# Attention matmuls of a two-block model kernel: operands padded to 128 rows and over 64 columns

## The chip, the cores and the metric

The kernel runs on one core of one Trainium2 chip. The metric is the device time of one execution in microseconds, as the median of three runs. One execution was also taken by the hardware profiler; its span runs from the first to the last instruction.

The engines are TensorE (PE; its weight loads are listed apart as PEld), VectorE (DVE), ScalarE (ACT), GpSimd (POOL) and SyncE (SP, which issues the weight transfers). A matmul has a stationary operand, loaded first by a weight load, and a moving operand that is streamed through. The profile gives a matmul's shape as rows*columns of the stationary operand, then the output: `64*128 64x464` uses 64 rows of the array, 128 of its columns and streams 464 columns.

## What is computed

Two blocks on 512 tokens of 1024 features. The first one is the place of the change: it puts 16 learned tokens in front, normalizes, projects to queries, keys, values, a gated linear unit and two gates, runs differential attention beside a causal depthwise convolution of 31 taps, mixes both, and ends with a feed-forward part. The second block (two layers of convolution and retention) isn't touched.

```python
def _diff_attention(q, k, v, lam, cid):
    ...
        s = jnp.einsum('bqhmd,bkhmd->bhmqk', qb, kf)
        mask = cid[None, :] <= qc[:, None]
        p = jax.nn.softmax(jnp.where(mask, s, NEG_INF), axis=-1)
        a = p[:, :, 0] - lam * p[:, :, 1]
        return jnp.einsum('bhqk,bkhe->bqhe', a, vf)
...
o = _diff_attention(q, k, v, lam, cid)
y_att = (_rms(o, subln_w[l]) * (1.0 - lambda_init)).reshape(b, lp, ATT_V)
...
m = jax.nn.sigmoid(g_att) * y_att + jax.nn.sigmoid(g_conv) * y_conv
```

Eight heads have two maps each (m = 0, 1) of 64 features; the softmaxes of the two maps are subtracted. A query sees the keys of its own chunk of 64 tokens and of those before it.

## The kernel before

All inputs are float32. A product is split: an operand becomes a high part (float32r) and a low part (the rest), and three products high x high, low x high and high x low are added up (`proj`, line 149). The weights come tile by tile: SyncE transfers 512 KB, ScalarE makes the high part (line 137), VectorE the low part (line 138), three tiles ahead of their use.

Features lie on the partitions for the projections, so a head's query tile has map 0 on partitions 0 to 63 and map 1 on 64 to 127. For the scores, four transfers on GpSimd's queue copy the high part of each map onto both halves of the partitions (`qh`, line 479), and four more build `kk` (line 492): for map 0 the high part of the keys over the low part, for map 1 the low part over the high part. One matmul of 128 rows (`qh` on `kk`, lines 523 and 535) then adds high x high and high x low at once. The third product, the low part of the query on the high part of the key, has 64 rows only: partitions 0 to 63 for map 0, 64 to 127 for map 1 (`MAP`, lines 527 and 536).

The queries of a head are worked on in five tiles (`QT`): 66, 128, 128, 128 and 64 queries with 80, 208, 336, 464 and 528 keys. In tiles 0 to 3 the first rows must not see the last 64 keys; a matmul adds -1e30 there, with `ones_r` of 2 or 64 columns as the stationary operand (line 526). In tile 4 the scores of a map fill two pieces of 264 keys, so it takes four matmuls (lines 535, 536). Then VectorE takes the maximum (lines 529, 538), ScalarE the exponential (line 544), VectorE subtracts the maps (line 550), TensorE transposes the result block by block (line 554) and ScalarE copies it (line 557). The output is a sum over blocks of keys (line 565); float32 there makes two passes of each matmul. The last block has 16 keys, so 16 rows. A sum over the features of the squared output, for the norm, uses one column of ones (line 572) and is copied to one row of `ssq` for each head (line 574); head 7 uses all columns of ones.

In the same loop stand the projections of values, queries, keys and gates. The depthwise convolution is VectorE work (line 389), put behind the rest in priority, and so are the normalization of its result (`norm_1`, `norm_2`) and the last gates. After the heads come the convolution's output product (line 587) and, between its parts, two matmuls with `sel` that spread 1 / rms of a head over all partitions (line 596). A planner lays out each engine's order once, before the run; engines then work through their lists in order and wait for each other by semaphores.

Of the kernel before, what the change touches and what calls it, by code (L numbers as in the profile page):

```python
# [18 lines left out]
P = 128  # L19
# [43 lines left out]
def kernel(ctx, tc, hT, par, pos, decay, w1, w2, out):  # L63
# [11 lines left out]

    # ---------------------------------------------------------------- weights
    order = []
# [71 lines left out]
    def proj(ps, w, xh, xl, t0, n, nk=NK, first=True, last=True, late=0):  # L149
        """ps[128, n] (+)= w^T x over nk blocks of 128 rows, in three float32r passes; the last  # L150
        late blocks after all others."""
        wh, wl = w
        passes = ((wh, xh), (wl, xh), (wh, xl))
        steps = [(a, b, k) for r in (range(nk - late), range(nk - late, nk)) for a, b in passes for k in r]
        for i, (a, b, k) in enumerate(steps):
            PE.matmul(ps, lhsT=a[:, ks(k)], rhs=b[k][:, t0:t0 + n],  # L156
                      start=first and i == 0, stop=last and i == len(steps) - 1)
# [4 lines left out]

    # ---------------------------------------------------------------- constants
    pr = const.tile([P, NPAR], F32, name="pr")
# [17 lines left out]
    def later(steps, by=20000):  # L182
        """Steps that fill gaps: behind the others of the attention in the scheduler's eyes."""
        at_ = tc.cur_priority
        tc.cur_priority = at_ + by
        steps()
        tc.cur_priority = at_

    # ---------------------------------------------------------------- norms
    class SumSq:  # L190
        """Per lane sums of squares over feature tiles, as the tiles come."""

# [14 lines left out]
        def total(self, ps, c0, cn, more=None):  # L207
            """The sum over all features, on every partition, with the squares of one more tile."""
            PE.matmul(ps, lhsT=ones, rhs=self.acc[:, c0:c0 + cn], start=True, stop=more is None)
            if more is not None:  # L210
                sq = npool.tile([P, T1], F32, tag="ntmp", bufs=3, name=f"sqx_{self.tag}_{c0}")
                S.activation(sq[:, :cn], more, AF.Square)
                PE.matmul(ps, lhsT=ones, rhs=sq[:, :cn], start=False, stop=True)
            return ps

        def by_token(self, ps, t0, col):
            """The sums of 128 tokens, a token on each partition."""
            PE.matmul(ps[:, col:col + 2], lhsT=self.acc[:, t0:t0 + P], rhs=ones[:, 0:2], start=True, stop=True)
# [13 lines left out]

    # =============================================================== block 1
    mixs = ExitStack()
# [21 lines left out]
    for c0, cn in C528:  # L256
# [4 lines left out]
        if c0 == 0:  # L261
            nc.sync.dma_start(pr[:, 8:], par[:, 8:])
    # also as h w, without 1 / rms: the first products don't wait for it
    xu = [[hpool.tile([P, T1], F32R, tag=f"x{p}", name=f"xu{p}{k}") for k in range(NK)] for p in "hl"]
# [22 lines left out]

    # u carries 1 + tanh(x / 2) = 2 sigmoid(x), so the taps are halved
    cw = pr[:, PAR["conv_dw_w"]:PAR["conv_dw_w"] + 8 * CONV_K]
# [34 lines left out]

    # ---- attention
    atts = ExitStack()
# [25 lines left out]
    later(lambda_, LB)  # L352

    negrow = ap1.tile([P, 64], F32R, name="negrow")
    V.tensor_scalar(negrow, ones[:, 0:64], ident[:, 0:1], NEG, ALU.mult, ALU.mult)
# [3 lines left out]
    for i in range(2):  # L359
        v_ = ap1.tile([P, 5, 256], F32, name=f"v{i}")  # L360
        V.memset(v_[:, 4, :], 0.0)
        vt.append(v_)
    ql_t = []
    for i in range(1):
        q = ap1.tile([P, 2, TQ], F32R, name=f"ql{i}")
        ql_t.append(q)
    at = []
# [51 lines left out]
    V.tensor_scalar(subw, pc("subln_w"), 0.5 * (1.0 - LAMBDA_INIT), None, ALU.mult)  # L419
    sel = mpool.tile([P, 4, P], F32R, name="sel")  # L420
    for j in range(4):
        V.tensor_scalar(sel[:, j, :], ones, ident[:, 32 * j:32 * j + 1], None, ALU.mult)
    tgc = []
# [23 lines left out]
    def att_rstd(tags):  # L447
        """1 / rms of the outputs of some heads, a head on a row, in two parts."""
        hi, lo = [ap1.tile([P, T1], F32R, tag=tag, name=f"rstd_{tag}")[:, :TQ] for tag in tags]
# [3 lines left out]
    for h in range(HEADS):  # L453
# [3 lines left out]
        if h % 2 == 0:  # L457
            wa, wb = getw(), getw()
            for tb in range(5):
# [7 lines left out]
                S.copy(vt[(h // 2) % 2][:m, tb, :], ps)  # L467
        # q: the high parts of each map twice, on both halves of the partitions
        w = getw()
        qh = ap2.tile([P, 2, TQ], F32R, tag="qh", bufs=1, name=f"qh{h}")  # L470
        qf, ql = ql_t[0][:, 0], ql_t[0][:, 1]
        for i, (c0, cn) in enumerate(C514):
            ps = mmA(f"q{h}_{i}")[:, :cn]
            proj(ps, w, xh, xl, TQ0 + c0, cn)
            c = slice(c0, c0 + cn)
            split(ps, qf[:, c], ql[:, c])
        for m in range(2):
            for r in range(2):
                nc.gpsimd.dma_start(fv(qh[64 * r:64 * r + 64, m, :]), fv(qf[64 * m:64 * m + 64, :]))
        # k: high part over low part (map 0), low part over high part (map 1)  # L480
        w = getw()
# [33 lines left out]
        for t, (q0, qn, nkey) in enumerate(QT):  # L515
# [3 lines left out]
            if t < 4:  # L519
                ps = psS.tile([P, 2, 512], F32, tag="ps", name=f"s{h}_{t}")  # L520
                nw = nkey
                for m in range(2):
                    PE.matmul(ps[:qn, m, :nw], lhsT=qh[:, m, q0:q0 + qn], rhs=kk[:, m, :nw], start=True, stop=False)
                    # the first rows don't see the last block of keys: -1e30 there
                    hid = HALO if t == 0 else 64
                    PE.matmul(ps[:hid, m, nkey - 64:nkey], lhsT=ones_r[:, :hid], rhs=negrow, start=False, stop=False)
                    PE.matmul(ps[:qn, m, :nw], lhsT=ql[MAP[m], q0:q0 + qn], rhs=kk[MAP[m], m, :nw], start=False, stop=True)
                    pm.append(ps[:qn, m, :nkey])
                V.tensor_reduce(mx[:qn], ps[:qn, :, :nkey], AX.X, ALU.max)
            else:  # L530
                for m in range(2):
                    ps = psS.tile([P, 1024], F32, tag="ps", name=f"s{h}_{t}_{m}")
                    for c0, cn in C528:
                        o = 248 + c0
                        PE.matmul(ps[:qn, o:o + cn], lhsT=qh[:, m, q0:q0 + qn], rhs=kk[:, m, c0:c0 + cn], start=True, stop=False)
                        PE.matmul(ps[:qn, o:o + cn], lhsT=ql[MAP[m], q0:q0 + qn], rhs=kk[MAP[m], m, c0:c0 + cn], start=False, stop=True)
                    pm.append(ps[:qn, 248:248 + T1])
# [4 lines left out]
            for m in range(2):  # L542
# [8 lines left out]
                                   ALU.mult, ALU.subtract)  # L551
            ptr = psT.tile([P, 512], F32, tag="tr", name=f"tr{h}_{t}")
            for b in range(nb):
                PE.transpose(ptr[:, b * qn:(b + 1) * qn], at[t][:qn, b * P:(b + 1) * P], ident[:qn, :qn])
            src = ptr[:, :nb * qn].rearrange("p (b q) -> p b q", b=nb)
            aT, qo = (aTA, q0) if t < 2 else (aTB, q0 - 194)
            S.copy(aT[:, :nb, qo:qo + qn], src)

        for aT, q0, qn, blocks in (
            (aTA, 0, 194, ((0, 0, P), (1, 66, P))),  # L560
            (aTB, 194, 320, ((0, 0, P), (1, 0, P), (2, 0, P), (3, 128, P), (4, 256, META))),
        ):
# [8 lines left out]
            if h < HEADS - 1:  # L571
                PE.matmul(ps[0:1, :qn], lhsT=ones[:, 0:1], rhs=sq[:, :qn], start=True, stop=True)
                g, r = SSQ[h]
                S.copy(ssq[r:r + 1, q0:q0 + qn], ps[0:1, :qn])
            else:
# [4 lines left out]

    # ---- m = sigmoid(g_conv) * y_conv + sigmoid(g_att) * y_att, in og
    for n in range(NK):
# [28 lines left out]

    # ---- h = h + m @ w_out
    res, res2 = [], []
# [18 lines left out]

    # ---- FFN
    psF = ctx.enter_context(tc.tile_pool(name="psF", bufs=PSF[0], space=PSUM, reuse_waits="tile"))
# [24 lines left out]
    def rotary():  # L659
# [12 lines left out]
        for dst, q in ((sn, 0.0), (cs, 0.25)):  # L672
# [8 lines left out]
            S.activation(dst, dst, AF.Sin)  # L681
        # lower half negated: -x2 sin there, x1 sin on the upper half
        V.tensor_scalar(sn[0:64], sn[0:64], -1.0, None, ALU.mult)
# [51 lines left out]

    # =============================================================== block 2
    b2pool = ctx.enter_context(tc.tile_pool(name="b2pool", bufs=1, reuse_waits="tile"))

    # rstd of the layer's input norm: by token (rt) and on every partition (rs). The first layer's
    # input is the final norm of block 1, so its own norm's square of rstd is 1 / (b + eps (a + eps))  # L740
    # on the raw sums, a = mean h^2 and b = mean (h w)^2.
    for l in range(2):
# [38 lines left out]
        for h in range(HEADS):  # L781
# [38 lines left out]
            if h == 0:  # L820
                # as the halves of x come
                for c0, cn in HALF:
# [62 lines left out]
        for cc in range(NK):  # L885
            def ctile(tag, n=SEQ):
                # the first ones don't wait for the end of the retention
                if cc == 1 and tag == "yv":
# [76 lines left out]
        for n in range(NK - 2):  # L965
            job(n, 0, SEQ)
        # brings the table of Sqrt in ahead of the norm
        S.activation(tmp1, sso.acc[:, 0:1], AF.Sqrt)
# [84 lines left out]
```

## Time and profile before

| | |
|---|---|
| median of 3 runs | 1922.99 us (1922.12 to 1925.09) |
| span of the profiled execution | 1920.3 us |
| TensorE busy | 1898.4 us (99%), 11802 matmuls |
| weight loads busy | 1679.8 us (87%) |
| VectorE busy | 1303.0 us (68%) |
| ScalarE busy | 837.3 us (44%) |
| GpSimd busy | 76.3 us (4%) |
| chain that ended last | 97% TensorE |

Heads 0 to 7 and the mixing of both branches run from about 108 to 507 us, before them the gated linear unit, after them the output product, the feed-forward part and block 2.

How to read it: matmuls are pipelined, and the end of one is modelled, so its duration (say 0.28 us for 258 columns) is longer than the time it takes from its neighbours. The time a matmul takes in a stream is the distance from its start to the start of the next one. A line of the order of time that ends in x8 is eight matmuls in a row, and its first number is the start of the first. "idle before <-" in brackets is time in which that engine did nothing ahead of the instruction. The windows give the time in which an engine was busy in a stretch, and in brackets its instructions.

### The profile page before, as it was taken

How to read it: one execution, taken by the hardware profiler on the slowest of the kernel's cores; microseconds unless marked ns; L12 is line 12 of the kernel's file. 1: busy time of each engine (PE TensorE's matmuls, PEld its weight loads, DVE VectorE, ACT ScalarE, POOL GpSimd, SP SyncE). 2: the span in 40 equal slices, each digit the busy share in tenths (PEclk: the TensorE clock that was granted, in tenths of full speed). 3: DMA queues.
4: the chain of work that ended last, by engine and by line, in shares of the span. 5: the costliest groups of instructions: out<-in, count | busy, mean ns of one | idle time of the engine just before them, and what ended most of it. 6: DMA issues, size and time to landing. Idle time of an engine off the chain costs nothing.

```text
span 1920.3 us, 29228 instructions
## 1 busy us (share of the span) xinstructions
PE 1898.4 (99%) x11802; PEld 1679.8 (87%) x11802; DVE 1303.0 (68%) x2116; ACT 837.3 (44%) x1473; POOL 76.3 (4%) x123
## 2 busy tenths in 40 slices
PE   8999999999999999999999999999999999999997
PEld 7999888888999999988988888888898888888887
DVE  8998888667678777733588776454277877745424
ACT  7234454566345444433445553222255555422222
POOL 3000000110000000000000000000020000000000
PEclk9999999999999999999999999999999999999999
DMA  4232223332333222222223222222223222222221
GB/s 150 99 112 88 89 67 100 89 89 67 105 111 99 88 97 91 83 102 99 91 77 108 79 88 88 99 90 95 98 69 99 94 92 90 77 99 88 99 94 60
DMA packets 53047, 177.78 MB, mean 93 GB/s; under 512 B 6640, under 2 KB 10736, under 8 KB 52912
## 3 DMA queue, kind: packets, MB, share of 16 engines
q1 hardware_dynamic: 47696, 160.80, 25.2%
q0 software_dynamic: 5072, 15.10, 2.9%
q8 instruction: 93, 1.52, 0.3%
q14 instruction: 42, 0.34, 0.1%
q10 hardware_dynamic: 144, 0.00, 0.0%
HBM read 165.25 MB, written 2.10 MB: 87 GB/s over the span
## 4 chain that ended last, share of the span: by engine, by line
PE 97%; DVE 1%; ACT 1%; issue 0%; DMA 0%; POOL 0%; SPq 0%; DVEq 0%; POOLq 0%
PE up L156 13%; PE w L156 9%; PE dn L156 6%; PE rz L156 5%; PE cb L156 5%; PE cx L156 5%; PE cc L156 5%; PE cz L156 5%; PE rq L156 5%; PE rk L156 5%; PE rv L793 4%; PE v L466 3%; PE k L156 3%; PE q L156 3%; PE yc L156 2%; PE ga L156 2%
## 5 line engine op out<-in xcount | busy, mean ns | idle before, releaser
L137 ACT CAST wh<-wraw 128x1024 fp32r<-128x1024 f32 (+1 forms) x300 | 313.1, 1045 | 503.6 <-PE cx L156 69.0
L138 DVE TENSOR_TENSOR wl<-wraw,wh 128x1024 fp32r<-128x1024 f32 (+1 forms) x300 | 364.6, 1216 | 195.6 <-ACT wh L137 194.9
L389 DVE SCALAR_TENSOR_TENSOR y<-u,pr,y 128x514 f32<-128x514 f32 x240 | 170.2, 744 | 0.0
L156 PE MATMUL up<-xh_ffn,wh 128*128 128x258 f32 x704 | 99.0, 282 | 0.0
L156 PE MATMUL up<-xl_ffn,wh 128*128 128x258 f32 x704 | 98.6, 282 | 0.0
L156 PE MATMUL up<-xh_ffn,wl 128*128 128x258 f32 x704 | 98.5, 282 | 0.0
L156 PEld LDWEIGHTS up<-xh_ffn,wh 128*128 128x128 f32 x704 | 90.5, 189 | 0.1
L156 PEld LDWEIGHTS up<-xl_ffn,wh 128*128 128x128 f32 x704 | 90.4, 189 | 0.0
L156 PEld LDWEIGHTS up<-xh_ffn,wl 128*128 128x128 f32 x704 | 90.4, 189 | 0.0
L706 DVE SCALAR_TENSOR_TENSOR cv<-cg,pr,cv 128x256 f32<-128x256 f32 x176 | 83.8, 480 | 7.9 <-ACT cv L703 6.5
L703 ACT ACTIVATE cv<-cg,pr 128x256 f32<-128x256 f32 x88 | 52.8, 599 | 63.4 <-DVE cg L700 63.4
L156 PE MATMUL w<-ml,wh 128*128 128x512 f32 (+1 forms) x320 | 66.9, 350 | 0.0
L156 PE MATMUL w<-mh,wh 128*128 128x512 f32 (+1 forms) x320 | 66.6, 350 | 0.0
L156 PE MATMUL w<-mh,wl 128*128 128x512 f32 (+1 forms) x320 | 66.2, 349 | 0.0
L876 DVE RECIPROCAL rsq<-rsq 128x512 f32<-128x512 f32 x16 | 53.6, 3350 | 14.1 <-ACT rsq L875 14.1
L156 PEld LDWEIGHTS w<-mh,wh 128*128 128x128 f32 x320 | 52.6, 188 | 8.8
L156 PEld LDWEIGHTS w<-ml,wh 128*128 128x128 f32 x320 | 52.5, 188 | 8.8
L156 PEld LDWEIGHTS w<-mh,wl 128*128 128x128 f32 x320 | 52.2, 188 | 8.7
L700 DVE TENSOR_TENSOR cg<-up,rs_ffn 128x258 f32<-128x258 f32 x88 | 37.3, 425 | 12.8 <-PE up L156 12.7
L156 PE MATMUL dn<-dh,wh 128*128 128x512 f32 (+1 forms) x198 | 44.6, 365 | 0.0
L156 PE MATMUL dn<-dh,wl 128*128 128x512 f32 (+1 forms) x198 | 44.6, 365 | 0.0
L156 PE MATMUL dn<-dl,wh 128*128 128x512 f32 (+1 forms) x198 | 44.6, 365 | 0.0
(409 smaller groups left out, 4281.4 us busy)
## 6 DMA issues: line engine op xcount, KB each, us to landing
wraw<-w_in SPq DMA_DIRECT2D x160, 512.0 KB, 3.3
wraw<-w_up SPq DMA_DIRECT2D x44, 512.0 KB, 3.3
wraw<-w_out SPq DMA_DIRECT2D x40, 512.0 KB, 3.3
wraw<-w_v SPq DMA_DIRECT2D x24, 512.0 KB, 3.3
wraw<-w_down SPq DMA_DIRECT2D x16, 512.0 KB, 3.3
qh<-ql POOLq DMA_DIRECT2D x32, 128.5 KB, 2.8
wraw<-w_conv_out SPq DMA_DIRECT2D x8, 512.0 KB, 3.3
dc<-dec POOLq DMA_DIRECT2D x16, 256.0 KB, 3.1
```

What stands on the lines that cost most here:

```text
L137: S.copy(wh[:, :n], raw)
L138: V.tensor_tensor(wl[:, :n], raw, fv(wh[:, :n]), ALU.subtract)
L156: PE.matmul(ps, lhsT=a[:, ks(k)], rhs=b[k][:, t0:t0 + n], start=first and i == 0, stop=last and i == len(steps) - 1)
L389: V.scalar_tensor_tensor(ys[i][:, :TQ], src, wj, ys[i][:, :TQ], ALU.mult, ALU.add)
L466: PE.matmul(ps, lhsT=x, rhs=w, start=p == 0 and k == 0, stop=p == 2 and k == NK - 1)
L700: V.tensor_tensor(g, ps, rs[:, c * 256:c * 256 + 258], ALU.mult)
L703: S.activation(t, g[:, 0:256], AF.Identity, scale=pr[:, o:o + 1], bias=pc("ffn_dw_b", f))
L706: V.scalar_tensor_tensor(t, g[:, k:k + 256], pr[:, o:o + 1], t, ALU.mult, ALU.add)
L793: PE.matmul(ps, lhsT=xx, rhs=w, start=p == 0 and k == 0, stop=p == 2 and k == NK - 1)
L876: V.reciprocal(rr, rr)
```

## The change

The attention's matmuls are given 128 rows and over 64 columns:

- `ql`, the low part of the query, becomes two tiles of 128 partitions, one for each map, with zeros on the other map's half. The third product then runs over all rows of `kk`; the other half adds zero. VectorE makes the two halves in two instructions.
- The query tiles are two columns longer (zeros), so that tile 4 computes 66 rows of scores; only 64 are used.
- The stationary operand of the -1e30 matmul is `hide`: 64 columns of ones, 64 of zeros (for tile 0 its last 66 columns).
- Tile 4's transposes take 66 rows.
- The last block of keys in the output takes 128 rows; the rows beyond 16 are zero in both operands (the value tile is cleared there at the start).
- The sum of squares uses all 128 columns of ones; the head's row is then read out of the result.
- `sel` is made after the heads, in the buffer of `qh`.

```diff
+    hide = ap1.tile([P, P], F32R, name="hide")
+    V.tensor_copy(hide[:, 0:64], ones[:, 0:64])
+    zero(hide[:, 64:128])
...
+    qf = ap1.tile([P, TQ + 2], F32R, name="qf")
+    ql = ap1.tile([P, 2, TQ + 2], F32R, name="ql")
+    zero(qf[:, TQ:])
+    zero(ql[64:128, 0, :])
+    zero(ql[0:64, 1, :])
...
-            split(ps, qf[:, c], ql[:, c])
+            S.copy(qf[:, c], ps)
+            for m in range(2):
+                V.tensor_tensor(ql[MAP[m], m, c], ps[MAP[m]], fv(qf[MAP[m], c]), ALU.subtract)
...
-                    hid = HALO if t == 0 else 64
-                    PE.matmul(ps[:hid, m, nkey - 64:nkey], lhsT=ones_r[:, :hid], rhs=negrow, start=False, stop=False)
-                    PE.matmul(ps[:qn, m, :nw], lhsT=ql[MAP[m], q0:q0 + qn], rhs=kk[MAP[m], m, :nw], start=False, stop=True)
+                    hid = hide[:, 64 - HALO:] if t == 0 else hide
+                    PE.matmul(ps[:qn, m, nkey - 64:nkey], lhsT=hid, rhs=negrow, start=False, stop=False)
+                    PE.matmul(ps[:qn, m, :nw], lhsT=ql[:, m, q0:q0 + qn], rhs=kk[:, m, :nw], start=False, stop=True)
...
-                        PE.matmul(ps[:qn, o:o + cn], lhsT=qh[:, m, q0:q0 + qn], rhs=kk[:, m, c0:c0 + cn], start=True, stop=False)
-                        PE.matmul(ps[:qn, o:o + cn], lhsT=ql[MAP[m], q0:q0 + qn], rhs=kk[MAP[m], m, c0:c0 + cn], start=False, stop=True)
+                        PE.matmul(ps[:66, o:o + cn], lhsT=qh[:, m, q0:q0 + 66], rhs=kk[:, m, c0:c0 + cn], start=True, stop=False)
+                        PE.matmul(ps[:66, o:o + cn], lhsT=ql[:, m, q0:q0 + 66], rhs=kk[:, m, c0:c0 + cn], start=False, stop=True)
...
+            qw = max(qn, 66)
             for b in range(nb):
-                PE.transpose(ptr[:, b * qn:(b + 1) * qn], at[t][:qn, b * P:(b + 1) * P], ident[:qn, :qn])
+                PE.transpose(ptr[:, b * qw:(b + 1) * qw], at[t][:qw, b * P:(b + 1) * P], ident[:qw, :qw])
...
-            (aTB, 194, 320, ((0, 0, P), (1, 0, P), (2, 0, P), (3, 128, P), (4, 256, META))),
+            (aTB, 194, 320, ((0, 0, P), (1, 0, P), (2, 0, P), (3, 128, P), (4, 256, P))),
...
-                PE.matmul(ps[0:1, :qn], lhsT=ones[:, 0:1], rhs=sq[:, :qn], start=True, stop=True)
+                PE.matmul(ps[:, :qn], lhsT=ones, rhs=sq[:, :qn], start=True, stop=True)
                 g, r = SSQ[h]
-                S.copy(ssq[r:r + 1, q0:q0 + qn], ps[0:1, :qn])
+                S.copy(ssq[r:r + 1, q0:q0 + qn], ps[r:r + 1, :qn])
...
+    sel = ap2.tile([P, 4, P], F32R, tag="qh", bufs=1, name="sel")
+    for j in range(4):
+        V.tensor_scalar(sel[:, j, :], ones, ident[:, 32 * j:32 * j + 1], None, ALU.mult)
```

The lines that made `sel` before the heads are removed. The matmuls of the values' last 16 tokens keep their 16 columns. Comments are dropped as well.

## Rows read from the trace of the kernel before

**Rows 1.** Windows: stretch, its length, then busy time of each engine.

```profile
40.00:108.00 68.00, 68.00 (x564) 67.86 (x562) 64.87 (x100) 21.04 (x32) 0.00 (x0) 1.00 0.30 101
...
147.00:366.00 219.00, 219.00 (x1605) 191.57 (x1604) 184.48 (x349) 105.59 (x262) 20.45 (x40) 1.00 0.29 86
366.00:507.00 141.00, 140.94 (x1030) 125.69 (x1029) 95.62 (x185) 81.54 (x173) 9.29 (x18) 1.00 0.27 83
```

**Rows 2.** Chain of waits in order of time: start, length, what; feed-forward part.

```profile
560.93 246.40 PE up L156 x2059
```

**Rows 3.** Order of time on TensorE, a softmax tile of 464 keys: start, duration, what.

```profile
275.09 0.38 PE L523 MATMUL s<-kk,qh 128*128 128x464 f32 x1
275.30 0.19 PE L526 MATMUL s<-negrow,ones_r 128*64 128x64 f32 x1
275.43 0.47 PE L527 MATMUL s<-kk,ql 64*128 64x464 f32 x1
275.83 0.47 PE L523 MATMUL s<-kk,qh 128*128 128x464 f32 x1
276.14 0.19 PE L526 MATMUL s<-negrow,ones_r 128*64 128x64 f32 x1
```

**Rows 4.** The same stretch, weight loads.

```profile
275.09 0.14 PEld L526 LDWEIGHTS s<-negrow,ones_r 128*64 128x64 f32 x1
275.43 0.18 PEld L527 LDWEIGHTS s<-kk,ql 64*128 64x128 f32 x1 [0.20 <-issue]
```

**Rows 5.** Order of time on TensorE, matmuls of 128 columns in block 2.

```profile
986.10 0.28 PE L852 MATMUL st<-qh,kl 128*128 128x128 f32 x1
986.21 0.27 PE L852 MATMUL st<-ql,kh 128*128 128x128 f32 x1
```

**Rows 6.** Order of time on TensorE, tiles of 80 and 208 keys.

```profile
428.90 0.25 PE L527 MATMUL s<-kk,ql 64*66 64x80 f32 x1
429.08 0.36 PE L523 MATMUL s<-kk,qh 128*128 128x208 f32 x1
429.29 0.19 PE L526 MATMUL s<-negrow,ones_r 128*64 128x64 f32 x1
429.41 0.36 PE L527 MATMUL s<-kk,ql 64*128 64x208 f32 x1
429.70 0.39 PE L156 MATMUL gc<-xl_mix,wh 128*128 128x258 f32 x1
```

**Rows 7.** Order of time on TensorE, the tile of 528 keys.

```profile
202.94 0.28 PE L535 MATMUL s<-kk,qh 128*64 128x264 f32 x1
...
203.94 0.38 PE L156 MATMUL q<-xl_mix,wh 128*128 128x256 f32 x1
```

**Rows 8.** Order of time on TensorE, around a sum of squares.

```profile
297.86 1.13 PE L156 MATMUL k<-xh_mix,wh 128*128 128x264 f32 x8
298.93 0.70 PE L572 MATMUL pss<-osq,ones 128*1 128x320 f32 x2
299.55 1.24 PE L156 MATMUL k<-xh_mix,wl 128*128 128x264 f32 x8
```

**Rows 9.** Order of time on TensorE, an output over five blocks of keys.

```profile
204.16 2.46 PE L565 MATMUL po<-aTB,v 128*128 128x320 f32 x10
206.55 0.62 PE L156 MATMUL q<-xl_mix,wh 128*128 128x256 f32 x3
```

**Rows 10.** Order of time on TensorE, transposes of 64 rows.

```profile
231.38 0.52 PE L554 MATMUL tr<-ident,a 64*128 64x64 f32 x5
231.84 0.39 PE L156 MATMUL q<-xh_mix,wl 128*128 128x258 f32 x1
```

**Rows 11.** Groups on VectorE: shapes, count, busy us, mean ns.

```profile
L161 DVE TENSOR_TENSOR ql<-q,ql 128x258 fp32r<-128x258 f32 x8 | 3.3, 418 | 0.0
```

**Rows 12.** VectorE's waits, 147 to 366 us: us in total, times, longest.

```profile
DVE mx L529 <- PE s L527: 10.4, 14, 1.3
DVE mx L538 <- PE s L536: 5.8, 7, 2.0
```

More of the change, by code (lines that the diff above doesn't have):

```diff
@@ L362 @@
         vt.append(v_)
[L363 to L366, printed above, removed]
+    qf = ap1.tile([P, TQ + 2], F32R, name="qf")
[3 more added lines that the diff above has]
+    zero(ql[0:64, 1, :])
+    zero(ql[0:64, 0, TQ:])
+    zero(ql[64:128, 1, TQ:])
     at = []
@@ L419 @@
     V.tensor_scalar(subw, pc("subln_w"), 0.5 * (1.0 - LAMBDA_INIT), None, ALU.mult)
-    sel = mpool.tile([P, 4, P], F32R, name="sel")
-    for j in range(4):
-        V.tensor_scalar(sel[:, j, :], ones, ident[:, 32 * j:32 * j + 1], None, ALU.mult)
     tgc = []
@@ L469 @@
         w = getw()
-        qh = ap2.tile([P, 2, TQ], F32R, tag="qh", bufs=1, name=f"qh{h}")
-        qf, ql = ql_t[0][:, 0], ql_t[0][:, 1]
+        qh = ap2.tile([P, 2, TQ + 2], F32R, tag="qh", bufs=1, name=f"qh{h}")
         for i, (c0, cn) in enumerate(C514):
@@ L552 @@
             ptr = psT.tile([P, 512], F32, tag="tr", name=f"tr{h}_{t}")
+            qw = max(qn, 66)
             for b in range(nb):
-                PE.transpose(ptr[:, b * qn:(b + 1) * qn], at[t][:qn, b * P:(b + 1) * P], ident[:qn, :qn])
-            src = ptr[:, :nb * qn].rearrange("p (b q) -> p b q", b=nb)
+                PE.transpose(ptr[:, b * qw:(b + 1) * qw], at[t][:qw, b * P:(b + 1) * P], ident[:qw, :qw])
+            src = ptr[:, :nb * qw].rearrange("p (b q) -> p b q", b=nb)
             aT, qo = (aTA, q0) if t < 2 else (aTB, q0 - 194)
-            S.copy(aT[:, :nb, qo:qo + qn], src)
+            S.copy(aT[:, :nb, qo:qo + qn], src[:, :, :qn])
         for aT, q0, qn, blocks in (
             (aTA, 0, 194, ((0, 0, P), (1, 66, P))),
-            (aTB, 194, 320, ((0, 0, P), (1, 0, P), (2, 0, P), (3, 128, P), (4, 256, META))),
+            (aTB, 194, 320, ((0, 0, P), (1, 0, P), (2, 0, P), (3, 128, P), (4, 256, P))),
         ):
```

## The prediction

> **What bounds the kernel now.** I read the stretches first: in every stretch of the attention (108 to 507 us) TensorE is busy for all of it and its clock is granted in full, while VectorE, the next one, has gaps [rows 1]. So I asked what TensorE's time is made of, and for that the unit is not the busy time of a matmul (these overlap) but the distance from its start to the start of the next. The chain of waits gives the undisturbed price: 2059 matmuls of 258 columns in 246.40 us, 0.120 us each [rows 2]. The order of time of one softmax tile gives the disturbed one [rows 3]: a full-width matmul of 464 columns takes 0.21 us to the next start (275.09 to 275.30) when it comes after full-width work; the one with 64 rows takes 0.40 (275.43 to 275.83) for as many columns; and the next full-width one takes 0.31 (275.83 to 276.14) instead of 0.21. The weight loads say why [rows 4]: the load for the 64 columns of ones starts at 275.09, with the matmul before it still running, so it is hidden; the load for the 64-row matmul starts only at 275.43, together with its matmul, after 0.20 us in which no load ran. So a change of the number of rows costs two things, each way: the array runs empty (0.09 to 0.10 us), and the next weight load lies bare (0.10 us). A change to fewer columns alone (128 to 64) costs nothing that these rows show. The one exception is the one-column sum: there, too, both sides show the loss [rows 8].
>
> One floor limits what padding can gain: matmuls with few columns but 128 columns of weights come every 0.11 us [rows 5], the time of the load.
>
> **The change part by part.** "Before" is start to start; "after" is the undisturbed price: 0.12 for 258 to 264 columns, 0.21 for 464, 0.155 for 336 (between these two by columns), 0.11 wherever the floor is higher.
>
> 1. Scores of tiles 1 to 3: 8 heads x 2 maps x 3 = 48 groups of query high, ones, query low. Tile 3: low part 0.40 to 0.21, the exposed load after it 0.10 to 0, the ones 0.13 to 0.11 (128 columns of weights must now be loaded behind it): 0.31 saved [rows 3]. Tile 2 has the same losses at 336 columns: 0.31. Tile 1: 0.29 to 0.11 (floor), 0.21 to 0.11 for the next, 0.12 to 0.11: 0.29 [rows 5, 6]. Sum 16 x (0.31 + 0.31 + 0.29) = 14.6 us.
> 2. Tile 0 (66 queries), 16 groups: 0.18 for the low part and 0.10 bare behind it, where 429.08 to 429.29 is 0.21 and not 0.11 [rows 6]. After, the floor, since a full weight load follows: 0.11. Saved 0.17, sum 2.7 us. The first two of a group have 2 or 66 columns of weights now and 66 afterwards; I cost them at nothing (0.06 each way at most, half the floor, 1.0 us).
> 3. Tile 4 (64 queries), 16 groups of four: 202.94 to 203.94 is 1.00 us [rows 7] plus 0.10 bare behind; after, 4 x 0.12. Saved 0.62, sum 9.8 us.
> 4. The sums of squares of heads 0 to 6, 14 pairs, with 128 columns of weights in place of one: 0.09 in front (eight matmuls in 1.07 us, not 0.98), 0.09 in the pair (0.62 for two of 0.265), 0.10 bare behind as in rows 3 [rows 3, 8]. Saved 0.28, sum 3.9 us. The copy now reads row r instead of row 0: the same.
> 5. The output's last block, 8 times two passes of 16 rows: ten passes in 2.39 us [rows 9]; six of 320 columns at 0.265 and two of 192 at 0.16 leave 0.48 for these two. After, the floor twice, 0.22; bare load behind 0.10. Saved about 0.35, sum 2.8 us.
> 6. Transposes of tile 4, five each, 66 rows instead of 64: 0.46 now [rows 10], 0.09 in front, 0.10 behind. After 4 x 0.065 + 0.11 = 0.37 if their loads are as quick as now, 0.55 if the floor of rows 5 holds. Nearest is the same transpose two columns narrower, so 0.37: 0.28 saved, less where it follows 64-row work already: 2.0 us (0.6 at the other end).
>
> Sum 35.8 us of TensorE time; 33 to 37 with the ends above.
>
> What is added elsewhere: the low part of the queries is two subtractions on half the lanes instead of one; an instruction of 258 columns takes 418 ns [rows 11], and I take the same for half the lanes (less is possible), so 16 x 0.42 = 6.7 us of VectorE over the eight heads. Some 15 short fills of zeros at the start of the attention, 3 us by that row at most, once. The four queue-issued copies of a query tile stay four; a row is 8 bytes longer. They are issued on GpSimd's queue as before and still wait for both halves of the high part only. The selector for the norm moves behind the last scores, since it takes the query tile's buffer: four short VectorE steps, and its readers (14 pairs of matmuls between the products of the convolution) can't start before. These products can run in their place, so I cost it at nothing; if they were not there it would be about 2 us.
>
> What is late next. VectorE is busy 184.5 of 219 us between 147 and 366 us [rows 1], where the convolution fills its gaps. Five heads are computed there, so TensorE wants to save 5/8 of 35.8 = 22.4 us and VectorE gets 4.2 us more: 188.7 of 196.6 us, 96%. That is what it bears between 40 and 108 us (64.87 of 68, 95%) without TensorE stopping once [rows 1]. And 16.2 us of its idle time there is waiting for the scores that now come sooner [rows 12]. I take off 2 us here. After 366 us VectorE has 45 us to spare; there I take off 2.5 us, one head's gain on its scores, for the serial normalization of the convolution, which the first matmuls behind it need. Together 4.5 off: 31.3 us.
>
> Every later stage only starts earlier. 1920.3 - 31.3 = 1889.0 us of span; the median of the runs is 2.7 us above the span of the profiled execution, so **1891.7 us**.
>
> **The rivals.**
>
> VectorE becomes the bound of heads 0 to 4. For it: 96% leaves 7.9 us for all its waits on others. If only the waits on the scores vanish and all other idle time stays, VectorE needs 184.5 + 4.2 + (34.5 - 16.2) = 207 us, so 12 us are saved there instead of 22.4. Against: the convolution is filler, and 95% was borne before. With 2.5 off later: 35.8 - 10.4 - 2.5 = 22.9, **1900 us**.
>
> The change doesn't do what it says, and it is slower: a weight load stays uncovered whenever the array is still at work on the same rows, so that padded matmuls lie as bare as now. Its place is the 64 groups of scores and the 28 sums; its price is that the padded loads are longer, 64 or 127 more columns at 0.11 per 128: 64 x 0.055 + 28 x 0.11 = 6.6 us, with nothing gained: **1930 us**. It decides if full-width loads aren't hidden behind full-width matmuls. Against it stands [rows 4]: at 275.09 a load on all 128 rows runs under a matmul on all 128 rows. The Trainium skill has this rule, on the page "TensorE: Matmul & The Clock Gate", section "What overlaps and what doesn't": weight loads overlap running matmuls only when their row groups differ. By it, padding to all rows would be the wrong thing, and the loads of rows 2 would be bare at every matmul; this trace shows them hidden there (0.120 us start to start), so I give it little. The same page's other sentence (Part 2, step 1), that a load may also go to a background buffer, is the one these rows bear out.
>
> The order of the instructions is planned anew, and a wait lands where there was none (the scores behind their copies, the selector). Its price lies between the selector's 2 us and VectorE's 10 us above, off the gain, 1894 to 1902 us.
>
> **How the numbers follow.** Forecast 0.62 (1884 to 1894 us); VectorE as the bound 0.20 (1895 to 1903); new order 0.11; slower 0.04; the rest, half of the gain or less, 0.03. The range leaves out the slower case and the rest: its low end is 37 us saved and nothing lost (1886) with 3 us for an order that comes out better, its high end the second and third case with some of both, 1905. A measurement can tell about 0.2% (4 us) from no change; faster 0.93, same 0.03, slower 0.04.
>
> **What would show it.** Right: in one softmax tile of the changed kernel, the low part of 464 columns at about 0.21 us to the next start and no idle time before its weight load; tile 4's four at 0.49; attention some 31 us shorter; everything from 507 us on as long as before. TensorE's idle time inside the attention, now none, says how much VectorE or the new order gave back: under 5 us if I am right, over 10 if VectorE binds, with the transposes, the weights' low parts or the scores waiting for VectorE. Wrong: a load that still starts with its matmul.

## The result and the profile after

| | before | after |
|---|---|---|
| median | 1923.43 us (1922.12 to 1925.09, 4 runs) | 1901.85 us (1900.37 to 1902.45, 4 runs) |
| span of the profiled execution | 1920.3 us | 1900.5 us |
| TensorE busy | 1898.4 us (99%) | 1869.6 us (98%) |
| VectorE busy | 1303.0 us (68%) | 1312.2 us (69%) |

The ratio is 0.9889, 95% interval 0.9875 to 0.9903: 21.6 us faster. The range (1883 to 1905) holds the time. The likeliest case (31.7 us off, its own range 1884 to 1894) did not come; 1901.85 lies in the places of two rivals, VectorE as the bound (1895 to 1903) and a new order (1894 to 1902). The time alone can't tell them apart; the waits below do.

**The padding does to TensorE what the steps say.** Order of time on TensorE in the kernel after, a tile of 464 keys (start, duration, what), the counterpart of [rows 3]:

```profile
378.40 0.37 PE L529 MATMUL s<-kk,qh 128*128 128x464 f32 x1
378.60 0.19 PE L532 MATMUL s<-negrow,hide 128*128 128x64 f32 x1
378.63 0.45 PE L533 MATMUL s<-kk,ql 128*128 128x464 f32 x1
378.93 0.37 PE L529 MATMUL s<-kk,qh 128*128 128x464 f32 x1
```

378.40 to 378.93 is 0.53 us for a group; 275.09 to 275.83 in [rows 3] was 0.74, with the bare load behind it still to come. The forecast was 0.21 + 0.11 + 0.21. The ones take 0.03 and the low part 0.30: the floor is paid in another place, the sum is the same. The weight loads of the same tile, the counterpart of [rows 4], have no idle time before them:

```profile
378.40 0.19 PEld L532 LDWEIGHTS s<-negrow,hide 128*128 128x128 f32 x1
378.61 0.19 PEld L533 LDWEIGHTS s<-kk,ql 128*128 128x128 f32 x1
```

Tile 4, the counterpart of [rows 7], and a sum of squares, that of [rows 8], both on TensorE:

```profile
278.83 0.28 PE L541 MATMUL s<-kk,qh 128*66 128x264 f32 x1
278.95 0.28 PE L542 MATMUL s<-kk,ql 128*66 128x264 f32 x1
279.07 0.29 PE L541 MATMUL s<-kk,qh 128*66 128x264 f32 x1
279.19 0.28 PE L542 MATMUL s<-kk,ql 128*66 128x264 f32 x1
279.31 0.87 PE L156 MATMUL q<-xh_mix,wl 128*128 128x256 f32 x6
...
282.06 0.28 PE L156 MATMUL k<-xh_mix,wl 128*128 128x264 f32 x1
282.18 0.70 PE L579 MATMUL pss<-osq,ones 128*128 128x320 f32 x2
282.48 1.25 PE L156 MATMUL k<-xh_mix,wl 128*128 128x264 f32 x7
283.57 1.12 PE L156 MATMUL k<-xl_mix,wh 128*128 128x264 f32 x8
```

Four matmuls in 0.48 us (1.00 before), and the pair of the sum takes 0.30 to the next start (0.62 before). But that is not all of its price: the seven matmuls behind it take 1.09 us to the next start (282.48 to 283.57), where seven at 0.12 are 0.84. So some 0.25 us of the pair's time shows behind it, and it costs about 0.54. Before, it cost 0.62 and the 0.09 in front and 0.10 behind that the prediction names. So it saves about 0.28, as forecast, and not 0.32. The undisturbed price of the feed-forward part is what it was, as the chain of waits says:

```profile
541.85 246.40 PE up L156 x2059
```

**TensorE now stands still.** Windows of after (stretch, length, then busy us and instructions of PE, PEld, DVE, ACT, POOL; granted clock, DMA share, GB/s), to be held against [rows 1]; the last two rows are two stretches in which the granted clock was at the lower level, 1.2 GHz:

```profile
147.00:366.00 219.00, 218.01 (x1775) 212.38 (x1774) 202.73 (x388) 117.61 (x292) 24.54 (x48) 1.00 0.32 98
366.00:507.00 141.00, 133.19 (x1025) 128.43 (x1024) 99.14 (x193) 81.42 (x163) 6.79 (x13) 0.96 0.25 80
...
232.00:317.00 85.00, 85.00 (x684) 82.43 (x683) 81.41 (x156) 43.93 (x111) 8.17 (x16) 1.00 0.30 94
...
395.60:402.40 6.80, 5.78 (x23) 5.06 (x24) 3.81 (x3) 4.60 (x7) 0.00 (x0) 0.50 0.23 77
426.30:429.70 3.40, 3.40 (x18) 3.40 (x18) 3.40 (x6) 2.27 (x7) 0.00 (x0) 0.50 0.12 25
```

Before, TensorE never waited between 100 and 500 us. After, its waits there are these (us in total, times, longest). `gc` and `ga` are the projections of the two gates, `tgc` and `tga` what ScalarE makes of them, `lnv` the sum for the variance of the convolution's normalization, `rs_ln` one over its root, and `yc` the convolution's output product:

```profile
PE yc L156 <- ACT tgc L439: 2.7, 1, 2.7
PE lnv L209 <- ACT rs_ln L221: 2.2, 1, 2.2
PE yc L156 <- DVE tgc L599: 2.1, 2, 1.4
PE tr L561 <- ACT aTA L564: 1.0, 1, 1.0
PE gc L156 <- ACT tga L448: 0.5, 1, 0.5
PE pss L579 <- DVE og L576: 0.3, 1, 0.3
```

All but the 1.0 us lie behind 392 us, in the serial normalization of the convolution (`norm_2`) and what follows. Order of time on TensorE there:

```profile
392.18 0.60 PE L209 MATMUL lnv<-acc_ln,ones 128*128 128x258 f32 x2
393.11 0.81 PE L579 MATMUL pss<-osq,ones 128*128 128x320 f32 x2 [0.32 <-DVE og L576]
396.14 1.22 PE L209 MATMUL lnv<-acc_ln,ones 128*128 128x256 f32 x2 [2.23 <-ACT rs_ln L221]
397.83 2.09 PE L156 MATMUL gc<-xh_mix,wh 128*128 128x258 f32 x8 [0.48 <-ACT tga L448]
399.72 1.92 PE L156 MATMUL gc<-xh_mix,wl 128*128 128x258 f32 x8
...
425.54 1.51 PE L156 MATMUL yc<-xh_u,wh 128*128 128x258 f32 x8 [2.67 <-ACT tgc L439]
```

`norm_2` works on two halves of 258 and 256 tokens. Before, both sums were four matmuls in a row at 420.02. In the new order the second half comes 3.96 us behind the first, has to wait until ScalarE has read the first, and ScalarE reloads its table for it. ScalarE in that place:

```profile
394.31 1.28 ACT L221 ACT_TABLE_LOAD   x1
395.61 0.48 ACT L221 ACTIVATE rs_ln<-lnv,epsc 128x258 f32<-128x258 f32 x1
396.10 1.28 ACT L448 ACT_TABLE_LOAD   x1
397.40 0.66 ACT L448 ACTIVATE tga<-ga 128x258 f32<-128x258 f32 x2
398.08 0.42 ACT L581 COPY ssq<-pss 1x320 f32<-1x320 f32 x1
398.52 1.28 ACT L221 ACT_TABLE_LOAD   x1
399.81 0.48 ACT L221 ACTIVATE rs_ln<-lnv,epsc 128x256 f32<-128x256 f32 x1
```

The clock falls to half 1.7 us into the stand of 2.23 us, at 395.60, for 6.8 us: the eight `gc` matmuls at 397.83 take 1.89 us to the next start, where eight of 0.12 are 0.96. From the first `lnv` to the first `yc` it was 25.1 us (420.02 to 445.12), and is 33.4.

The longest stand, 2.67 us ahead of `yc`, ends with this instruction on ScalarE:

```profile
425.10 0.40 ACT L439 ACTIVATE tgc<-gc 128x256 f32<-128x256 f32 x1
```

`yc` doesn't read `tgc`, so what it waits for must be one of the three buffers that the projections share. In ScalarE's order that instruction stands behind eight casts of the normalized convolution, from 419.52 on, and the high part of a weight tile at 424.15.

**Where the 19.8 us of span come from.** Worked out from TensorE's order of time, first `v` to first `wo`, each matmul by the distance to the next start, idle time apart. The two columns on the right are two kernels of the last experiments, whose edits differ in the padding alone.

| us | before | after | g4 (not padded) | f1 (padded) |
|---|---|---|---|---|
| scores and -1e30 | 55.0 | 32.9 | 55.0 | 32.8 |
| `po` | 23.0 | 20.4 | 23.3 | 20.4 |
| `pss` | 7.8 | 4.4 | 7.8 | 4.2 |
| transposes | 9.8 | 8.6 | 10.0 | 8.7 |
| projections, norms, `rb`, `yc` | 303.4 | 303.5 | 307.0 | 300.5 |
| TensorE idle | 0.1 | 8.8 | 2.2 | 1.3 |
| sum | 399.1 | 378.6 | 405.3 | 367.8 |

Before to after, TensorE's work shrinks by 29.2 us (399.0 to 369.8, unrounded). That holds the loss from the clock: 5.78 us of busy time at 395.6 and 3.40 at 426.3, half of each lost, an estimate of 4.6 us. So the padding gave 33.8 us. Against it stand 8.7 us of added idle time, the 4.6 us, and 1.4 us lost at the start (first `v` at 109.71, not 108.30); later stages are 0.7 us shorter. 33.8 - 8.7 - 4.6 - 1.4 + 0.7 = 19.8.

### The profile page after: what moved, and what is told of

The parts are those of the page before. It is cut to its first block, busy times and chain, and to the rows that moved or that the text cites. A ratio compares the mean times of both kernels' runs of the same rounds, so it can differ in the third digit from the quotient of the medians.

```text
span 1900.5 us, 29258 instructions
## 1 busy us (share of the span) xinstructions
PE 1869.6 (98%) x11802; PEld 1683.7 (89%) x11802; DVE 1312.2 (69%) x2147; ACT 838.8 (44%) x1475; POOL 75.0 (4%) x123
## 4 chain that ended last, share of the span: by engine, by line
PE 95%; DVE 2%; ACT 1%; issue 1%; POOL 0%; DMA 0%; SPq 0%; DVEq 0%; ACTq 0%; POOLq 0%
PE up L156 13%; PE w L156 9%; PE dn L156 6%; PE rz L156 5%; PE cb L156 5%; PE cx L156 5%; PE cc L156 5%; PE cz L156 5%; PE rq L156 5%; PE rk L156 5%; PE rv L804 5%; PE v L471 3%; PE gc L156 3%; PE k L156 2%; PE wo L156 2%; PE q L156 2%
```

## The experiments

The first theory: the padding's gain is on TensorE in full, and the lost part is the planner's new order around the convolution's normalization, with the clock that falls behind the stands. The second: VectorE, at up to 96% in heads 0 to 4, gives back what TensorE gains. The medians of the kernel before beside these runs were 1922.1 to 1922.9 us.

**Without the normalization of the convolution.** In four kernels `norm_1` and `norm_2` are left out (n1: before, n2: after, n3: only the score lines padded, n4: only the sums, the last block and the transposes).

```diff
-            later(norm_2, N2)
...
-            later(norm_1, N1)
+            pass
```

> The kernel before without the layer norm and SiLU of the convolution branch (its products take the raw convolution), so that no serial chain stands between the last head and those products. The convolution on VectorE stays. First theory (TensorE's gain from padding is there in full, and what is missing is lost at that chain): about 1910 to 1920 us, since TensorE was busy all the time before and only four float32 pairs of matmuls go. Second theory (VectorE's longer work eats the gain): says the same of this one. It is the base of the next three.

> The changed kernel without that layer norm and SiLU. First theory: 33 to 36 us below n1 (the sum of TensorE's terms was 35.8), TensorE idle under 2 us in the attention. Second theory: still 19 to 23 us below n1, since the convolution and the second subtraction are both still VectorE's, with TensorE waiting for VectorE in heads 0 to 4.

> As n2, with the sums of squares, the last block of keys and the transposes of the last tile as before: only the scores are padded. First theory: 27 us below n1 (terms 14.6, 2.7, 9.8), 25 to 29. Second theory: 12 to 17, since all of VectorE's added work is here.

> As n1, with only the sums of squares (128 columns), the last block of keys (128 rows) and the transposes of the last tile (66 rows) padded; VectorE's work is as before. First theory: 8.7 us below n1 (terms 3.9, 2.8, 2.0), 7 to 10. Second theory: the same, as nothing is added on VectorE. If the one-column sum lost its time to something other than its columns, 4 us less.

Measured: n1 1921.07 us (ratio 0.9991, 0.9982 to 1.0000), n2 1890.71 (0.9832, 0.9816 to 0.9848), n3 1901.08 (0.9887, 0.9872 to 0.9902), n4 1912.74 (0.9949, 0.9935 to 0.9964). n1 is 1 us above the 1910 to 1920 that was expected. Leaving the normalization out gains nothing that can be measured in the kernel before and 11.1 us after. With it gone the padding is worth 30.4 us: less than the first theory's 33 to 36, far more than the second's. In n2 TensorE is idle for 3.9 us in the attention (under 2 were expected), and the clock does not fall there. By the tally, idle time left out, TensorE's work shrinks by 33.4 us from n1 to n2. n3 (20.0 below n1) lies between what both theories say: its work shrinks by 24.0 us, and it is idle for 4.2, the most of it for ScalarE's copies behind the transposes. n4 (8.3) is where it was expected, but n1 has a spell of 3.4 us at half clock at 1433 us that n4 has not, which makes up to 1.7 of it. So these four point at the stretch; they do not settle the size.

**One reciprocal root for both halves of the variance (f1), another place for the gates' products (f2), both (f3), and f2's edit in the kernel before (f4).** f1 also takes the sum out of the projections' buffers into one of the scores'. `GC_EARLY` is the number of heads that do one of the eight `gc` products each; the other products come at the end.

```diff
-        for i, (c0, cn) in enumerate(C514):
-            ps = mmA(f"lnv{i}")[:, :cn]
-            rstd(rs[:, c0:c0 + cn], ss.total(ps, c0, cn), D, epsc[:, 1:2])
+        ps = psS.tile([P, 1024], F32, tag="ps", name="lnv")
+        for c0, cn in C514:
+            ss.total(ps[:, 254 + c0:254 + c0 + cn], c0, cn)
+        rstd(rs[:, :TQ], ps[:, 254:254 + TQ], D, epsc[:, 1:2])
```

```diff
-GC_EARLY = 5
+GC_EARLY = 4
```

> The changed kernel; the variance of the layer norm is summed for all 514 tokens into one buffer of the scores instead of two of the three buffers of the projections, and its root and reciprocal are one instruction each instead of two. First theory (the gain is lost at the serial chain of the layer norm, where TensorE stands for 2.2 and 0.5 us and then runs at half clock for 6.8 us): 5 to 7 us below the changed kernel, 1895 to 1897 us, with no gap of over 1 us at the variance. Second theory (VectorE's longer work): within 2 us of the changed kernel.

> The changed kernel with GC_EARLY = 4 instead of 5: the gate projection of head 4 is done at the end, where it can run while the layer norm's chain is waited for. TensorE has the same work. First theory: the gap of 2.7 us ahead of the convolution's products goes, and the 1.7 us at half clock behind it: 1896 to 1899 us. Second theory: VectorE has 5.7 us less of TensorE's time in heads 0 to 4 to hide in, so no gain or up to 5 us slower.

> f1 and f2 together. First theory: both gains, 1890 to 1894 us, within 4 us of the changed kernel without the layer norm (1890.7). Second theory: as f2.

> The kernel before with GC_EARLY = 4. TensorE had no gap there, so by the first theory nothing is gained by the constant alone: within 2 us of 1922.4. If f2 gains and this one as much, the gain of f2 is not that of the gap.

Measured: f1 1890.17 us (0.9828, 0.9814 to 0.9843), f2 1895.74 (0.9856, 0.9841 to 0.9871), f3 1903.20 (0.9894, 0.9879 to 0.9909), f4 1930.76 (1.0042, 1.0028 to 1.0057). **f1 beats both kernels**: 32.7 us below before, 11.7 below after. That is 5 us more than the first theory gave it, since not only the stand at the variance went. f1's one stand of TensorE between 100 and 500 us (us in total, times, longest) and its sums in the order of time:

```profile
PE tr L562 <- ACT aTA L565: 1.0, 1, 1.0
...
391.25 1.03 PE L209 MATMUL lnv<-acc_ln,ones 128*128 128x258 f32 x4
```

Both halves stand in one row again, and the first `yc` comes at 413.93 instead of 425.54. In f1 the clock falls nowhere between 14.4 and 1881.5 us. VectorE is as busy in heads 0 to 4 as in after (its windows, 232 to 317 us), and TensorE has no gap beside it:

```profile
232.00:317.00 85.00, 85.00 (x686) 82.51 (x685) 81.35 (x158) 44.41 (x113) 8.16 (x16) 1.00 0.30 94
```

f2 gains 6.1 us, as the first theory had it. Its halves are parted too, the second `lnv` 3.98 us behind the first, but TensorE stands for 0.91 us only, and the clock doesn't fall there. So the cost is in the stands and the clock, not in the parting as such.

f3 and f4 missed. f3 has both edits and is slower than either, and than after: its halves stand in one row, but there are new gaps of 1.1, 1.7 and 1.4 us at 394, 440 and 467 us. So one root doesn't protect from a bad order elsewhere. f4, where one constant differs, is 7.9 us slower than before: its order also parts the two halves, with a stand of 1.89 us ahead of the second and 6.8 us at half clock from 419.7 us. So that order is no property of padded matmuls: a small edit elsewhere can bring it.

**What else the change touches: columns without rows (g1, on f1), VectorE's added work without the padding (g2, on before), f1's edit in the kernel before (g3), and g2 with that edit (g4).**

```diff
-                    PE.matmul(ps[:qn, m, nkey - 64:nkey], lhsT=hid, rhs=negrow, start=False, stop=False)
+                    PE.matmul(ps[:hid, m, nkey - 64:nkey], lhsT=hide[:, :hid], rhs=negrow, start=False, stop=False)
...
-                PE.matmul(ps[:, :qn], lhsT=ones, rhs=sq[:, :qn], start=True, stop=True)
+                nc_ = 64 if h < 4 else 16
+                PE.matmul(ps[:nc_, :qn], lhsT=ones[:, :nc_], rhs=sq[:, :qn], start=True, stop=True)
```

(g1; tile 4's matmuls go back to `q0:q0 + qn` in the same way. g2 has the diff of the change but for its matmuls, so `lhsT=ql[MAP[m], m, q0:q0 + qn], rhs=kk[MAP[m], m, :nw]`, 64 rows, the one-column sums, 16 rows in the last block and 64-row transposes.)

> The changed kernel with one reciprocal root for both halves of the variance, in which the row padding stays (low part of the queries, last block of keys, transposes) and the column padding is taken back: 64 columns again for the -1e30 matmul (2 in tile 0) and for tile 4's scores, and for the sums of squares 64 columns in heads 0 to 3 and 16 in heads 4 to 6. If only the rows matter, as the rows of before suggest for 64 columns: tile 4's four matmuls still come at 0.12 us each, the -1e30 matmul between its neighbours costs no more than with 128 columns, the pair of a 64-column sum costs 0.30 us as with 128 and that of 16 columns too or up to 0.28 us more; time 1890 to 1894 us, against 1890 for the same kernel with all columns. If columns under 65 cost like rows: 0.2 us for each of 64 groups of scores or 28 sums, so 1900 to 1908 us.

> The kernel before with only the work that the change puts on VectorE: two subtractions per query piece in place of one, the fills of zeros, the selector made behind the heads; all matmuls as before. If VectorE's added work costs nothing, as the gap-free heads 0 to 4 of the changed kernel say: within 4 us of before (a new order may add or take that much). If VectorE was short: 5 to 10 us slower, with TensorE's waits for VectorE in heads 0 to 4.

> The kernel before with one reciprocal root for both halves of the convolution's variance, nothing else. If the 12 us that this edit gains in the changed kernel are the stands that its order had there, it gains nothing here, where TensorE has none: within 3 us of before. If the edit is worth as much by itself: 1909 to 1913 us, and the changed kernel's lost part isn't explained by its order.

> The kernel before with the change's work on VectorE (as g2_vector_side_only, 1936.1 us) and one reciprocal root for both halves of the variance (which gained nothing in the kernel before: 1921.9 us). If the change's lost part is the place where its order puts the two halves of the variance, the 14 us of g2 go away here as 12 us went away in the changed kernel: 1920 to 1926 us, and the padding alone is worth what lies between this and the changed kernel with one root, 32 to 34 us. If the added work on VectorE, or the later selector, costs by itself: 1931 to 1937 us, and the padding alone is worth over 40 us, which its terms on TensorE (33.6 us) don't hold.

Measured: g1 1900.12 us (0.9881, 0.9865 to 0.9898), g2 1936.11 (1.0070, 1.0055 to 1.0085), g3 1921.92 (0.9998, 0.9989 to 1.0007), g4 1926.98 (1.0022, 1.0013 to 1.0032).

g3: the edit that gains 11.7 us in the changed kernel gains nothing in the kernel before, as the first theory has it. f1's gain was the stands and the clock, not a cheaper norm. Whether the single instruction or the other buffer made that order possible was not tried apart.

g2 fits neither expectation, and it is the run that says most. With every matmul as before, the change's other edits cost 14.0 us (1936.11 against 1922.13 beside it). VectorE is not short: it has 190.05 us of work in the 219 us of heads 0 to 4, and TensorE is busy for 218.44 of them. TensorE's waits between 30 and 530 us (the largest; us in total, times, longest), and the two sums in the order of time:

```profile
PE tr L561 <- ACT aTA L564: 2.3, 3, 1.3
PE yc L156 <- DVE tgc L599: 1.4, 1, 1.4
...
419.61 0.60 PE L209 MATMUL lnv<-acc_ln,ones 128*128 128x258 f32 x2
...
423.34 1.22 PE L209 MATMUL lnv<-acc_ln,ones 128*128 128x256 f32 x2 [0.37 <-ACT rs_ln L221]
```

The halves are parted here as well, and the first `yc` comes 33.1 us behind the first `lnv`, as in after (33.4). None of the waits is for the added instructions (the two subtractions or the selector). It is the order that came with them: from the first `v` to the first `wo` 16.0 us more than before, of which 6.9 are idle, some 4.7 (an estimate) lost to the clock (6.8 us from 423.2 and 3.4 us from 477.8 at the lower level, less the idle time in them, halved) and 4.4 spread over several lines.

g4 came out at 1926.98, just beyond the first theory's 1920 to 1926: 9.1 us of g2's loss go away with one root. Of the 4.6 us left above the kernel before, 2.1 are idle (1.38 of it a wait of the scores for an exponential) and up to 1.7 a spell at half clock at 317.5 us. The padding alone is then g4 to f1, 36.8 us (32 to 34 were expected), and g2 to after, 34.3 us. Each of these pairs still has two orders in it.

g1 was expected at 1890 to 1894 if columns cost nothing and at 1900 to 1908 if they cost like rows; 1900.12 falls in the second, but the rows below give other reasons. Order of time on TensorE, tile 4 with 64 columns, and a sum of squares with 16, then the weight load behind that sum:

```profile
198.44 0.28 PE L542 MATMUL s<-kk,qh 128*64 128x264 f32 x1
198.56 0.28 PE L543 MATMUL s<-kk,ql 128*64 128x264 f32 x1
198.68 0.29 PE L542 MATMUL s<-kk,qh 128*64 128x264 f32 x1
198.80 0.28 PE L543 MATMUL s<-kk,ql 128*64 128x264 f32 x1
...
363.65 0.63 PE L156 MATMUL ga<-xh_mix,wl 128*128 128x256 f32 x4
364.21 0.71 PE L581 MATMUL pss<-osq,ones 128*16 128x320 f32 x2
364.86 0.74 PE L156 MATMUL ga<-xh_mix,wl 128*128 128x256 f32 x4
...
364.85 0.54 PEld L156 LDWEIGHTS ga<-xh_mix,wl 128*128 128x128 f32 x4 [0.53 <-issue]
```

Tile 4 loses nothing with 64 columns: 0.12 us each. The sum with 16 columns takes 0.65 us to the next start, the load behind it starts only with its matmul, and a sum with 64 columns does the same. With what shows in front of a pair and behind it, 16 or 64 columns cost some 0.3 us more than 128. By the tally all sums take 8.3 us in g1, 4.2 in f1 and 7.8 in before. So columns matter for the sums alone: some 4 of g1's 10.0 us. Most of the rest is order again: 5.9 us idle (1.3 in f1), with one stand of 2.7 us and 6.8 us at half clock that begin in it. In g1 TensorE also waits for the change's added instructions, 0.7 us for a subtraction and 0.4 us for the selector.

**All runs together.** With the normalization in place, the five kernels with all rows padded (after, f1, f2, f3, g1) lie between 1890 and 1903 us, the five with the rows unpadded (before, f4, g2, g3, g4) between 1922 and 1936. So the padding's gain stands clear of the order, while small edits and the orders that came with them move a kernel by 13 to 14 us on either side. f1 is the fastest of five, not what the padding must give.

## Why the prediction was right or wrong

**The reading of the bound: right.** TensorE's price is the distance between starts, a change of rows costs the empty array and the bare load, and both are gone after. One start alone can mislead, though: 0.03 us for the ones and 0.30 for the pair of a sum leave part of their time to the matmul behind.

**The sum of 35.8 us: right within 2.5 us.** TensorE's work, idle time left out, shrank by 33.8 us before to after, by 33.4 from n1 to n2, and by 36.5 from g4 to f1, of which up to 1.7 is g4's spell at half clock. By groups (g4 to f1): the scores' own lines 22.2, `po` 2.9, `pss` 3.6, transposes 1.3, and 6.5 in the other lines, where the bare loads lay and where g4's spell is. The terms of the scores (27.1 together) came out at 24.0 in n3, those of the rest (8.7) at 7.3 in n4's tally. The sums of squares, taken from [rows 8] as the exception to "fewer columns cost nothing", are one indeed, with 16 and 64 columns too (g1).

**Two subtractions in place of one: right in size.** 0.42 us each was taken; VectorE's group of half-lane subtractions has this row in after:

```profile
L482 DVE TENSOR_TENSOR ql<-q,qf 64x258 fp32r<-64x258 f32 x16 | 6.8, 422 | 0.6 <-PE s L533 0.2
```

**VectorE as the bound of heads 0 to 4 (0.20): it did not come.** The 2 us taken off for it were 1.0: one stand, for a copy by ScalarE. VectorE's waits for the scores shrank as foreseen. Its load went to 93% from 147 to 366 us (202.73 of 219) and to 96% from 232 to 317 us (81.41 of 85) without stopping TensorE there. The sign that was to tell, TensorE's idle time, came out between its two marks (under 5, over 10) at 8.8 us; what decides is that no wait in heads 0 to 4 is for VectorE. VectorE's waits in 147 to 366 us, against [rows 12]; the same stretch holds a tenth more matmuls than before:

```profile
DVE mx L535 <- PE s L533: 2.5, 3, 1.0
DVE mx L544 <- PE s L542: 0.2, 1, 0.2
```

**The step that failed is what is late next, behind 366 us.** I took 2.5 us off there for the serial normalization. Measured: 7.8 us idle and 4.6 us at half clock in the attention, and 1.4 us at the start. I had seen the right place but priced it as a chain that merely comes late, in the old order; the old order's two halves in a row were taken for granted. The selector, costed at nothing, and the two subtractions, costed by VectorE's load, were priced as instructions and not as a reason for a new plan: g2 loses 14.0 us with these edits without one wait on any of them. The mechanism is the third rival's, a new order with waits where there were none, which had a chance of 0.11 and a price of 2 to 10 us beyond the 4.5 taken off. What was given back is 14 us (8.7 idle, 4.6 by the clock, 1.4 at the start, less 0.7), so the time came out at the very end of that rival's 1894 to 1902. The fall of the clock stands in no term of the prediction. The range held the time because it was drawn over the second and the third rival.

**The slower rival: it did not come.** At 378.61 a load on all 128 rows starts under a running matmul on all rows, and no idle time stands ahead of it. The Trainium skill, page "TensorE: Matmul & The Clock Gate", section "What overlaps and what doesn't", lets weight loads overlap only where row groups differ; these rows disagree, as [rows 4] did.

The Trainium skill, page "TensorEngine Tiling (Array Packing)", section "Key Properties", says that a change of tiling mode drains TensorE. The trace agrees for rows (0.09 to 0.10 us in front of a matmul of 64 rows), and for the float32 sums of 16 and 64 columns (some 0.3 us a pair); it disagrees for tile 4's float32r matmuls of 64 columns on 128 rows, which come at 0.12 us each (g1).

**What stays open.** Which of the change's small edits on VectorE turns the order was not tried apart, nor whether the sums lose by their float32 type, nor which part of f1's edit restores the row of four. The 4.4 us that g2 loses beside its stands and the clock have no named place, and why f3's order is worse than that of either edit alone was not found.

## What to carry to other kernels

Price a TensorE edit by the distance between starts, over enough matmuls that what one leaves to the next is counted, and pad rows where full-row work surrounds a matmul: it gave the sum within 2.5 us. But where a planner lays out the order, put a term of its own in the sum for a new plan, with the serial chains listed (here a variance in two halves that could be parted), and look for a small edit that makes such a chain whole: the one-root edit was worth nothing before and 11.7 us after. It is no guarantee, since with one more constant changed it was worth nothing (f3, 1903.20 us), so try several orders before the price of a change is read. A kernel with only the side edits (g2 here) tells a lost gain from a cost that the main edit brings.

## What the runs showed of the hardware

- The granted clock fell to 1.2 GHz in or right behind stands of 2.23, 2.57 (at the start) and 2.67 us in after, and 2.72 us in g1, for 3.4 or 6.8 us. Stands of 2.09 us in before and 2.34 us in n1, both at 16 us, were not followed by it, one of 1.89 us in f4 was, and a spell of 3.4 us also came where TensorE had not stood at all (317.5 us in g4, 363.4 us in g3). In after it cost an estimated 4.6 us in the attention beside the stands themselves.
- Columns cost something in one kind of matmul here and nothing in another: 64 columns come at 0.12 us each for float32r scores as 66 do, and cost some 0.3 us more than 128 for a pair of float32 sums.
- A change of table on ScalarE took 1.28 us each time; three fell within 5.5 us, two of them ahead of results that TensorE waited for.
